# A hybrid decoder trunk on one core: constants first, x in pieces, merges in lockstep, and the second recurrence carried into the output projection

## The chip, the cores and the metric

The kernel runs on one core of one Trainium2 chip. The metric is the time of one execution in microseconds (us). TensorE (PE) multiplies matrices, PEld is its weight load, VectorE (DVE), ScalarE (ACT) and GpSimd (POOL) are the vector engines, and SyncE (SP) issues every DMA of this kernel. Each engine works off its own list of instructions in order.

## What is computed

Two layers over x of 1024 tokens by 1024 features, all float32, and a final RMSNorm. Cut to what matters:

```python
def hybrid_layer(x, ...):
    h = rms_norm(x, norm1_g)
    proj = h @ w_in              # q, k, v, z (4 heads of 128), b, a (4 + 4), short conv (3 x 512)
    qkv = silu(causal_depthwise_conv(qkv, dn_conv_w))
    q, k = l2_normalize(q), l2_normalize(k)
    beta, g = sigmoid(b_in), -exp(dn_a_log) * softplus(a_in + dn_dt_bias)
    o_dn = chunk_gated_delta_rule(q, k, v, g, beta)
    o_dn = o_dn * rsqrt(mean(o_dn * o_dn) + EPS) * dn_norm_g * silu(z)
    y = gate_b * causal_depthwise_conv(gate_c * hv, sc_conv_w)
    o_sc = y * rsqrt(mean(y * y, per group) + EPS) * sc_norm_g
    x = x + concatenate([o_dn, o_sc]) @ w_out
    h2 = rms_norm(x, norm2_g)
    return x + (silu(h2 @ w_gate) * (h2 @ w_up)) @ w_down      # 2816 wide
```

The gated delta rule runs over chunks of tokens one after the other: each step needs the state S that the step before it left.

## The kernel before

Activations lie transposed, features on partitions, tokens in two halves of 512. Every large product is made of three matmuls of 512 columns (`mm3`, L186): each operand is split into a rounded part hi (a cast, mostly on ACT) and the rest lo (a subtraction on DVE or POOL), and hi by hi, lo by hi and hi by lo are summed. So each weight block and each activation tile has to pass two engines before PE may use it.

A layer goes through these stages. The input projection takes head 0's k, q and v of half 0, then the decay inputs `ba` (tile ba_ps), then half 1, then heads 1, z of heads 0 and 1, the short convolution (`sconv`, products csc, hsc and bsc), heads 2 and 3, more `sconv`, z of heads 2 and 3. In layer 0 the second half of x is transposed (`x_half1`, tile xtp) and normed before `ba`, in one piece. Per head and half `gram` makes two products (gk, gq) and the tiles U and A; `value_tok` turns v round (vtok). A group of two heads is then a job: `invert` inverts small triangular blocks on DVE, DMAs carry them through DRAM, `merge` (rp, yp) puts the blocks together, `chain` runs four recurrence steps per half for its two heads (kS, TR, SU, op), `finish` norms and `gate` multiplies with z and stores the result to `od`.

Jobs run beside the projections: a job is a generator, `spawn` starts it with a lag, and `tick`, called at each matmul of a projection, moves it on when its lag is over. Then comes `drain()`, which runs all jobs to their end, and the output projection `po`: its operands are read back from DRAM (`ot`, and `rb`, the short convolution's norm factors, from `rd`), multiplied (L999) and split into `hhi_o` (ACT, L1000) and `hlo_o` (DVE, L1001), 8 tiles for each half of the tokens. After half 0's eight output blocks the second norm (sp_n, rr_n, bc) scales eight tiles xh (DVE, L1043) and splits them into hi_hP (ACT) and lo_hP (POOL) for the first two of the seven products P1 to P7 by which gate, up and down projections are made. Then half 1.

What stands on an engine in which order is decided by a list scheduler from the program's order, the pools' buffers (the `ot` tiles have 4) and dependencies.

Of the kernel before, what the change touches and what calls it, by code (L numbers as in the profile page):

```python
# [17 lines left out]
P = 128  # L18
# [10 lines left out]
LAG, TOK_LAG, SC_LAG, INV_LAG, GATE_LAG = 6, 36, 30, 110, 10  # L29
# [22 lines left out]
def tile_hybrid(ctx, tc, x, norm1_g, w_in, dn_conv_w, dn_a_log, dn_dt_bias, dn_norm_g,  # L52
# [18 lines left out]
          "Y": 4, "ub": 1, "yb": 1, "tb": 1, "X": 1, "R": 2, "rr0": 1, "rr1": 1, "vn0": 1, "vn1": 1, "St": 6}  # L71
# [159 lines left out]
    def w_in_early(l):  # L231
# [21 lines left out]
    xts = []  # L253
    for c in range(4):
        xt = sb(("ub", "yb")[c], f"xt_{c}", (P, D)) if c < 2 else \
            ring.tile([P, D], F32, tag=("whi", "wlo")[c - 2], bufs=3, name=f"xt_{c}")
        dma(xt, x[0, c * P:(c + 1) * P, :])
        xts.append(xt)
    split_early = w_in_early(0)
# [9 lines left out]
    xp = [[None, None] for _ in range(4)]
    for c in range(4):  # L270
        for kk in range(2):
            xp[c][kk] = sb(("k", "q")[kk], f"xp_{c}_{kk}")
            dma(xp[c][kk], x[0, HALF + c * P:HALF + (c + 1) * P, kk * HALF:(kk + 1) * HALF])
# [17 lines left out]
    for st, cst, n in ((st1, cst1, n_st1), (st2, cst2, n_st2)):  # L291
        ps = ps_("aux", "cps")
        PE.transpose(ps[:, :n], st, ident[:n, :n])
        V.tensor_copy(cst, ps[:, :n])
# [5 lines left out]
    def x_half1():  # L300

        s2x = sm.tile([P, 4, 2], F32, tag="ss1", bufs=1, name="ss1_1")
        for c in range(4):
            for kk in range(2):
# [24 lines left out]
    for l in range(DEPTH):  # L329

        if True:
# [21 lines left out]
            def ba():  # L353
# [3 lines left out]
                tp2 = fx(f"ba_tp{nm}", (P, NC, 16))  # L357
                for half in range(2):
# [5 lines left out]
                    S.copy(rows, ps)  # L364
                    for c in range(4):
                        PE.transpose(tp2[:, half * 4 + c, :], rows[:, c * P:(c + 1) * P], ident[:16, :16])
# [42 lines left out]
                V.tensor_scalar(neta, neta, -1.0, None, ALU.mult)  # L409

# [68 lines left out]
            def sumsq(ps, dst, nm):  # L479

                sq = sb("sqp", f"sq{nm}", sh4)
# [124 lines left out]
            def merge(hd, half, slot):  # L606

                nm = f"{l}_{hd}_{half}"
                U = units[hd, half]["U"]
# [4 lines left out]
                dma(Y, full_ap(yd[slot]))  # L614

                rp = aux(f"rp32_{nm}", (P, 4, 32))
# [8 lines left out]
                yp = aux(f"yp32_{nm}", (P, 2, 4, 32))  # L625
# [10 lines left out]
                rp = aux(f"rp64_{nm}", (P, 4, 64))  # L636
# [5 lines left out]
                yp = aux(f"yp64_{nm}", (P, 4, 64))  # L642
# [7 lines left out]
            def chain(g, half):  # L650
# [60 lines left out]
                yield GATE_LAG  # L711
                for hd in hds:
                    gate(hd, half)
# [51 lines left out]
            def sc_norm():  # L765
# [4 lines left out]
                r = rsqrt(m, [P, 32], f"r_{nm}", "s")  # L770
# [494 lines left out]
```

## Time and profile before

| what | value |
|---|---|
| median of 3 runs | 2458.01 us (2455.85 to 2458.72) |
| profiled execution: its time, its span | 2455.2 us, 2453.5 us |
| PE busy, share of the span | 2351.7 us, 96% |
| DVE, ACT, POOL busy | 1650.9, 915.9, 747.2 us |
| mean granted clock of TensorE | 0.985 |

The span is the time from the first to the last instruction. A granted clock of 1.00 is 2.4 GHz, 0.50 is 1.2 GHz. Matmuls are pipelined, so a busy PE is not a PE at its peak.

### The profile page before, as it was taken

Reading aid. Unit: us, or ns where it says so; the run is one execution under the profiler, and the core shown is the slowest. Engines: PE = TensorE matmul, PEld = TensorE weight load, DVE = VectorE, ACT = ScalarE, POOL = GpSimd, SP = SyncE. Lnnn points to the kernel's source line nnn. Section 1 sums busy time; section 2 is a strip of 40 time slices with the busy share of each in tenths; the row PEclk is TensorE's granted clock in tenths of the full one; section 3 lists DMA queues with packets and bytes.
Section 4 is the critical chain, followed back from the end, with each engine's and each line's share of the span. In section 5 each row is a group of like instructions: output and inputs, shape, how many; then the busy total and the mean of one; then the engine's idle time right before and its main releaser. Section 6 shows DMA issues by size and latency. Waiting matters only on the chain.

```text
span 2453.5 us, 31881 instructions
## 1 busy us (share of the span) xinstructions
PE 2351.7 (96%) x11522; PEld 1908.7 (78%) x11522; DVE 1650.9 (67%) x2786; ACT 915.9 (37%) x1933; POOL 747.2 (30%) x556
## 2 busy tenths in 40 slices
PE   6999999998999999899999999999999999999998
PEld 4787787786888888677867778888778888877777
DVE  7775763668566566797767666646776666568974
ACT  6524523434323223333344244244432232333334
POOL 3000000034454453456321001000445455434470
PEclk8999999999999999999999999999999999999999
DMA  7222222752342333644322312337324233255431
GB/s 225 72 62 75 64 68 82 224 155 64 100 129 91 111 110 96 205 142 140 116 69 72 73 48 69 75 105 243 104 86 129 90 104 111 92 179 167 134 120 69
DMA packets 360086, 274.16 MB, mean 112 GB/s; under 512 B 47310, under 2 KB 293368, under 8 KB 359928
## 3 DMA queue, kind: packets, MB, share of 16 engines
q1 hardware_dynamic: 359928, 272.13, 36.5%
q8 instruction: 90, 1.47, 0.3%
q14 instruction: 68, 0.56, 0.1%
HBM read 197.03 MB, written 75.04 MB: 111 GB/s over the span
## 4 chain that ended last, share of the span: by engine, by line
PE 77%; DVE 8%; issue 6%; DMA 3%; ACT 3%; POOL 2%; SPq 1%; POOLq 0%; DVEq 0%; ACTq 0%
PE P_g L186 16%; PE P_u L186 15%; PE P_d L186 10%; PE po L186 6%; PE ps_csc L186 4%; PE ps_bsc L186 4%; PE ps_hsc L186 4%; PE pd L186 3%; PE ps_q L186 2%; PE ps_v L186 2%; PE ps_z L186 2%; PE ps_k L186 2%; DMA stP<-hs_P 1%; POOL lo_dP L874 1%; DVE lo_hP L874 1%
## 5 line engine op out<-in xcount | busy, mean ns | idle before, releaser
L186 PE MATMUL P_g<-lo_hP,hiP_g 128*128 128x512 f32 x616 | 241.7, 393 | 8.5 <-DVE lo_hP L874 6.5
L186 PE MATMUL P_u<-hi_hP,hiP_u 128*128 128x512 f32 x616 | 241.8, 393 | 6.9 <-ACT hiP_u L898 6.9
L186 PE MATMUL P_g<-hi_hP,hiP_g 128*128 128x512 f32 x616 | 240.6, 391 | 1.3 <-ACT hiP_g L898 1.3
L186 PE MATMUL P_u<-lo_hP,hiP_u 128*128 128x512 f32 x616 | 241.2, 391 | 0.0
L186 PE MATMUL P_u<-hi_hP,loP_u 128*128 128x512 f32 x616 | 241.1, 391 | 0.0
L186 PE MATMUL P_g<-hi_hP,loP_g 128*128 128x512 f32 x616 | 240.1, 390 | 0.0
L186 PE MATMUL P_d<-lo_dP,hiP_d 128*128 128x512 f32 x504 | 202.5, 403 | 17.5 <-POOL lo_dP L874 14.6
L186 PE MATMUL P_d<-hi_dP,hiP_d 128*128 128x512 f32 x504 | 202.4, 403 | 9.5 <-ACT hi_dP L873 6.9
L186 PE MATMUL P_d<-hi_dP,loP_d 128*128 128x512 f32 x504 | 199.0, 396 | 1.6 <-DVE loP_d L899 1.6
L1173 DVE TENSOR_TENSOR xT<-P_d,xT 128x512 f32<-128x512 f32 x192 | 127.0, 682 | 50.7 <-PE P_d L186 48.5
L874 POOL TENSOR_TENSOR lo_hP<-xh,hi_hP 128x512 fp32r<-128x512 f32 x24 | 37.2, 1576 | 383.8 <-ACT hi_hP L873 383.8
L186 PEld LDWEIGHTS P_g<-lo_hP,hiP_g 128*128 128x128 f32 x616 | 115.9, 188 | 38.2 <-DVE lo_hP L874 11.0
L186 PEld LDWEIGHTS P_u<-hi_hP,hiP_u 128*128 128x128 f32 x616 | 116.7, 189 | 32.3 <-ACT hiP_u L898 7.8
L186 PEld LDWEIGHTS P_g<-hi_hP,hiP_g 128*128 128x128 f32 x616 | 115.9, 188 | 27.1 <-ACT hiP_g L898 2.2
L186 PEld LDWEIGHTS P_u<-lo_hP,hiP_u 128*128 128x128 f32 x616 | 116.8, 190 | 24.4
L186 PEld LDWEIGHTS P_u<-hi_hP,loP_u 128*128 128x128 f32 x616 | 116.5, 189 | 24.2
L186 PEld LDWEIGHTS P_g<-hi_hP,loP_g 128*128 128x128 f32 x616 | 115.9, 188 | 23.3
L186 PEld LDWEIGHTS P_d<-lo_dP,hiP_d 128*128 128x128 f32 x504 | 97.6, 194 | 46.0 <-POOL lo_dP L874 19.9
L186 PEld LDWEIGHTS P_d<-hi_dP,hiP_d 128*128 128x128 f32 x504 | 97.6, 194 | 36.2 <-ACT hi_dP L873 10.7
L898 ACT CAST hiP_g<-m_g 128x1024 fp32r<-128x1024 f32 (+1 forms) x66 | 60.1, 910 | 175.2 <-PE P_g L186 100.7
L898 ACT CAST hiP_u<-m_u 128x1024 fp32r<-128x1024 f32 (+1 forms) x66 | 60.1, 911 | 170.7 <-PE P_u L186 87.8
L186 PEld LDWEIGHTS P_d<-hi_dP,loP_d 128*128 128x128 f32 x504 | 96.5, 191 | 22.2 <-DVE loP_d L899 2.8
(393 smaller groups left out, 6069.1 us busy)
## 6 DMA issues: line engine op xcount, KB each, us to landing
stP<-hs_P SPq DMA_DIRECT2D x126, 256.0 KB, 3.8
m_g<-in_ffn_w_gate_dram SPq DMA_DIRECT2D x44, 512.0 KB, 3.9
m_u<-in_ffn_w_up_dram SPq DMA_DIRECT2D x44, 512.0 KB, 3.9
hs_P<-t SPq DMA_DIRECT2D x72, 256.0 KB, 2.2
m_d<-in_ffn_w_down_dram SPq DMA_DIRECT2D x48, 384.0 KB, 3.7
hs_P<-c_u SPq DMA_DIRECT2D x70, 256.0 KB, 2.4
raw_o<-in_w_out_dram SPq DMA_DIRECT2D x32, 512.0 KB, 4.8
xd<-xT SPq DMA_DIRECT2D x32, 256.0 KB, 2.4
```

Of the source, the lines that this page charges most:

```text
L186: last_mm[0] = PE.matmul(ps, lhsT=w(k)[i], rhs=m(k)[j], start=k + i + j == 0, stop=k + i == n).ins
L874: eng.tensor_tensor(res[1], src, res[0].bitcast(F32), ALU.subtract)
L898: S.copy(hi, src)
L1173: V.tensor_tensor(t, ps, t, ALU.add)
```

## The change

The constants' seven DMAs are issued ahead of x and their two transposes (cps) stand first on PE. The second half of x is loaded ahead of the first v weight, and `x_half1` is a job that moves on between projection matmuls. The first k weight's lo part is made on DVE in place of POOL. `ba` becomes a job behind half 0 of head 0. Both halves' `gram` come before `value_tok`. `merge` of the two heads of a group runs in lockstep, each with its own bank. `gate` is spawned with a lag of 40. `sconv(1)` moves ahead of head 2, `sconv(2)` and `sconv(3)` behind head 3. `drain()` moves from the end of the input projection to a place between the halves of the output projection, whose matmuls now tick the jobs, and the operands of half 1 (`load_os(1)`) are made behind it. In the first step of gate and up the products' order changes.

```diff
-LAG, TOK_LAG, SC_LAG, INV_LAG, GATE_LAG = 6, 36, 30, 110, 10
+LAG, TOK_LAG, SC_LAG, INV_LAG, GATE_LAG = 6, 36, 30, 114, 40
...
-          "Y": 4, "ub": 1, "yb": 1, "tb": 1, "X": 1, "R": 2, "rr0": 1, "rr1": 1, "vn0": 1, "vn1": 1, "St": 6}
+          "Y": 4, "ub": 1, "yb": 1, "tb": 1, "X": 2, "R": 2, "rr0": 1, "rr1": 1, "vn0": 1, "vn1": 1, "St": 6}
...
-        for c0, name, eng in ((512, f"k{l}_0", G), (0, f"q{l}_0", G), (1024, f"v{l}_0", G)):
+        for c0, name, eng in ((512, f"k{l}_0", V), (0, f"q{l}_0", G), (1024, f"v{l}_0", G)):
+            if between and len(raws) == 2:
+                between()
             t = ring.tile([P, KD, P], F32, tag="raw", bufs=3, name=f"raw_{name}")
...
-    xts = []
-    for c in range(4):
-        xt = sb(("ub", "yb")[c], f"xt_{c}", (P, D)) if c < 2 else \
...
-    split_early = w_in_early(0)
     dma(st1[0:DEPTH * 8, :], norm1_g.rearrange("l (k p) -> (l k) p", p=P))
...
+    xts = []
+    for c in range(4):
...
+    def load_half1():
+        for c in range(4):
+            for kk in range(2):
+                xp[c][kk] = sb(("k", "q")[kk], f"xp_{c}_{kk}")
+                dma(xp[c][kk], x[0, HALF + c * P:HALF + (c + 1) * P, kk * HALF:(kk + 1) * HALF])
+
+    split_early = w_in_early(0, load_half1)
...
+    for st, cst, n in ((st1, cst1, n_st1), (st2, cst2, n_st2)):
+        ps = ps_("aux", "cps")
+        PE.transpose(ps[:, :n], st, ident[:n, :n])
...
-    def x_half1():
+    def x_half1(hs):
...
+                yield 5
...
+        yield 10
+        hs[1] = make_h(lambda k: xT[1][k], r, lambda k: c_norm1(0, k), ps_("fx", "bc_n1_0_1"), "n1_0_1")
...
+                    rows2.append(rows)
+                return ba_rest(nm, rows2)
+
+            def ba_rest(nm, rows2):
+
...
+                for half in range(2):
+                    decay(0, half)
...
+                mb = (aux, fx)[hd % 2]
...
+                yield 14
+
+                rp = mb(f"rp32_{nm}", (P, 4, 32))
                 for c in range(4):
...
-                yield GATE_LAG
                 for hd in hds:
-                    gate(hd, half)
+                    spawn(call(gate, hd, half), GATE_LAG)
...
+                yield 16
...
+                if l + hd == 0:
+                    x_job = spawn(x_half1(hs), 8)
...
-                            hs[1] = x_half1()
-                        ba()
-                        decay(0, 0)
-                    if ty == "v" and hd + half > 0:
+                            while x_job in jobs:
+                                move(x_job)
...
-                        value_tok(hd, half)
-                        yield 24
+                        yield 8
                     if group is not None:
                         spawn(group, 0)
+                    for half in range(2):
+                        value_tok(hd, half)
+                        yield 12
...
-                    for hd in (2 * g, 2 * g + 1):
-                        yield from merge(hd, half, (hd % 2) * 2 + half)
+                    for lag in zip(*[merge(hd, half, (hd % 2) * 2 + half) for hd in (2 * g, 2 * g + 1)], strict=True):
+                        yield lag[0]
...
+            sconv(1)
             head(2, None)
             head(3, group(1))
-            for g in range(1, 4):
-                sconv(g)
-            spawn(call(sc_norm), SC_LAG + 12)
+            sconv(2)
+            sconv(3)
+            spawn(sc_norm(), SC_LAG + 12)
             w = [split_w(wcols(1536 + hd * P), f"z{l}_{hd}") for hd in (2, 3)]
...
-            drain()
...
-            for half in range(2):
+
+            def load_os(half):
...
+            load_os(0)
...
+                if half == 1:
+                    drain()
+                    load_os(1)
...
-                    mm3(ps, lambda k: (wo[0][:, korder[k], :], wo[1][:, korder[k], :]), lambda k: os_[half][k], KD)
+                    mm3(ps, lambda k: (wo[0][:, korder[k], :], wo[1][:, korder[k], :]), lambda k: os_[half][k], KD, tick)
...
-                        for it in (p0, p0, p1, p0, p1, p1):
+                        for it in (p0, p0, p0, p1, p1, p1):
...
-                    for qs in (("P1", "P2"), ("P5",), ("P6",), ("P7",), ("P3",), ("P4",)):
-                        if qs[0] in ("P4",):
-                            last_opnds(qs[0])
+                    for qs in (("P1", "P2"), ("P5", "P6"), ("P7", "P3", "P4")):
                         for m in mats[:2]:
                             for q in qs:
+                                if q == "P4" and m is mats[0]:
+                                    last_opnds(q)
                                 m.step(q)
                 elif i > 1:
...
```

**What the order of instructions shows.** Three places.

On PE, layer 0, where half 0 of the output projection ends (po_0_7 is its last block, po_1_0 the first of half 1; sp_n is the second norm's sum), the order of before goes on like this:

```order
L186 MATMUL po_0_7_4961<-hhi_o_0_7_4604,lo_o_7_4882 128x512
L864 MATMUL sp_n_0_0_4992<-ones_83,acc_0_0_4690 128x1
L186 MATMUL po_1_0_5078<-hhi_o_1_0_4610,hi_o_8_4919 128x512
L186 MATMUL po_1_0_5078<-hlo_o_1_0_4611,hi_o_8_4919 128x512
L186 MATMUL po_1_0_5078<-hhi_o_1_0_4610,lo_o_8_4920 128x512
L186 MATMUL po_1_0_5078<-hhi_o_1_1_4616,hi_o_8_4919 128x512
```

There po_1_0 needs hhi_o_1 and hlo_o_1, which DVE made while half 0's first four blocks ran. In this piece one sp_n is followed by half 1 at once. After the change eight sp_n and four bc stand between po_0_7 and po_1_0 on PE, and on DVE at the same place the operands of half 1 come behind the norm of half 0 (rsqrt, then eight scalings xh, of which the last five stand here):

```order
L1072 SCALAR_TENSOR_TENSOR xh_0_6_4555<-xh_0_6_4555,cst_88,bc_0_4958 128x512
L1072 SCALAR_TENSOR_TENSOR xh_0_1_4550<-xh_0_1_4550,cst_88,bc_0_4958 128x512
L1072 SCALAR_TENSOR_TENSOR xh_0_3_4552<-xh_0_3_4552,cst_88,bc_0_4958 128x512
L1072 SCALAR_TENSOR_TENSOR xh_0_5_4554<-xh_0_5_4554,cst_88,bc_0_4958 128x512
L1072 SCALAR_TENSOR_TENSOR xh_0_7_4556<-xh_0_7_4556,cst_88,bc_0_4958 128x512
L1026 SCALAR_TENSOR_TENSOR hlo_o_1_0_5004<-ot_1_0_5005,cst_89,hhi_o_1_0_5003 128x512
L1026 SCALAR_TENSOR_TENSOR hlo_o_1_1_5010<-ot_1_1_5011,cst_89,hhi_o_1_1_5009 128x512
L1026 SCALAR_TENSOR_TENSOR hlo_o_1_2_5016<-ot_1_4_5017,cst_89,hhi_o_1_2_5015 128x512
L1026 SCALAR_TENSOR_TENSOR hlo_o_1_3_5025<-ot_1_5_5026,cst_89,hhi_o_1_3_5024 128x512
L1024 TENSOR_TENSOR ot_1_6_5035<-ot_1_6_5035,rb_1_6_5037 128x512
```

All of half 1's operands have moved from the middle of half 0 to behind its scaling; on ACT the eight casts hi_hP stand ahead of the first hhi_o_1 likewise. The last four `ot` of half 1 are loaded into the buffers of the first four, and layer 1 has the same order.

On DVE, layer 0, before the change, the second half's normed tiles (ht_n_0_1) come behind the convolution of v (y_v, vT_v):

```order
L461 SCALAR_TENSOR_TENSOR y_v_0_0_579<-pre_v_0_0_576,cst_88,y_v_0_0_579 128x512 x3
L464 SCALAR_TENSOR_TENSOR vT_v_0_0_574<-pre_v_0_0_576,y_v_0_0_579 128x512
L211 SCALAR_TENSOR_TENSOR ht_n_0_1_0_702<-xT_0_245,cst_88,bc_n_0_1_695 128x512
L211 SCALAR_TENSOR_TENSOR ht_n_0_1_1_708<-xT_1_246,cst_88,bc_n_0_1_695 128x512
L211 SCALAR_TENSOR_TENSOR ht_n_0_1_2_714<-xT_2_247,cst_88,bc_n_0_1_695 128x512
L213 TENSOR_TENSOR hlo_n_0_1_0_701<-ht_n_0_1_0_702,hhi_n_0_1_0_700 128x512
```

After the change the ht_n_0_1 have moved ahead of it, to behind q's; the last of them and what follows:

```order
L211 SCALAR_TENSOR_TENSOR ht_n_0_1_5_691<-xT_5_256,cst_88,bc_n_0_1_654 128x512
L211 SCALAR_TENSOR_TENSOR ht_n_0_1_6_697<-xT_6_257,cst_88,bc_n_0_1_654 128x512
L213 TENSOR_TENSOR hlo_n_0_1_4_684<-ht_n_0_1_4_685,hhi_n_0_1_4_683 128x512
L211 SCALAR_TENSOR_TENSOR ht_n_0_1_7_703<-xT_7_258,cst_88,bc_n_0_1_654 128x512
L213 TENSOR_TENSOR hlo_n_0_1_6_696<-ht_n_0_1_6_697,hhi_n_0_1_6_695 128x512
L477 COPY halocv_0_744<-pre_v_0_0_745 128x3
L479 SCALAR_TENSOR_TENSOR y_v_0_0_748<-pre_v_0_0_745,cst_88,y_v_0_0_748 128x512
L472 COPY pre_q_0_1_914<-halocq_0_631 128x3
L479 SCALAR_TENSOR_TENSOR y_v_0_0_748<-pre_v_0_0_745,cst_88,y_v_0_0_748 128x512 x2
```

On PE, layer 0, in the output projection's second block (po_0_1), the change puts the second group's recurrence of half 1 (TR, SU, op, kS of heads 2 and 3) and the short convolution's transposed norm (rt_sc):

```order
L697 MATMUL TR_2_1_0_4344<-rr_2_1_0_4318,Y_2_1_4148 128x128
L697 MATMUL TR_3_1_0_4348<-rr_3_1_0_4323,Y_3_1_4153 128x128
L792 MATMUL rt_sc_4369<-ident,y_r_sc_4298 32x128
L186 MATMUL po_0_1_4659<-hhi_o_0_0_4477,lo_o_1_4546 128x512
L705 MATMUL SU_2_1_0_4358<-vn_2_1_0_4346,kdec_2_1_2775 128x128
```

So one matmul of po_0_1 stands between pieces of the recurrence here. Before, all four heads' recurrence and rt_sc stood ahead of the first po matmul.

## Rows read from the trace of the kernel before

**Rows 1.** Windows (us): busy time and instructions of each engine, granted clock, DMA.

```profile
core 0: us, PE busy (x) PEld busy (x) DVE busy (x) ACT busy (x) POOL busy (x), PEclk, DMA share, GB/s
0.00:26.00 26.00, 10.31 (x55) 9.77 (x55) 17.88 (x50) 12.52 (x31) 11.06 (x19) 0.80 0.86 259
...
47.00:64.00 17.00, 12.29 (x43) 4.68 (x43) 12.28 (x17) 7.52 (x19) 5.48 (x4) 0.80 0.33 123
...
200.00:300.00 100.00, 95.50 (x691) 76.00 (x690) 65.32 (x174) 52.90 (x192) 4.80 (x9) 0.98 0.21 57
...
375.00:450.00 75.00, 74.44 (x575) 59.53 (x575) 33.42 (x105) 28.29 (x111) 0.00 (x0) 1.00 0.31 90
...
504.60:518.90 14.30, 14.30 (x76) 12.04 (x75) 11.14 (x24) 7.95 (x13) 5.61 (x5) 1.00 0.32 101
```

**Rows 2.** Waits of PE, 0 to 65 us: us in total, times, longest.

```profile
PE cps L293 <- DMA xp<-in_x_dram: 5.7, 1, 5.7
PE cps L293 <- DMA st<-in_dn_conv_w_dram: 5.0, 1, 5.0
```

**Rows 3.** Timeline of the start: start us, us, engine, line, operation, xcount [idle before].

```profile
10.95 0.42 SPq L262 DMA_DIRECT2D st<-in_dn_conv_w_dram  x1
11.98 2.35 POOL L177 TENSOR_TENSOR lo_k<-raw_k,hi_k 128x1024 fp32r<-128x1024 f32 x1 [0.63 <-ACT hi_k L176]
12.03 2.32 DVE L155 TENSOR_TENSOR t_n<-y_n 128x4 f32<-128x4 f32 x1
14.47 5.69 DVE L156 TENSOR_TENSOR t_n<-t_n,rr_n 128x4 f32<-128x4 f32 x1
25.89 0.49 PE L186 MATMUL ps_k<-hhi_n,hi_k 128*128 128x512 f32 x1
```

**Rows 4.** Timeline of PE, 94 to 99 us.

```profile
98.15 0.66 PE L488 MATMUL vtok<-ident,vT_v 128*128 128x128 f32 x4 [2.77 <-DVE U L565]
```

**Rows 5.** Waits of PE, 1225 to 1330 us (layer 1).

```profile
PE vtok L488 <- DVE U L565: 4.5, 1, 4.5
PE ps_k L186 <- POOL lo_k L177: 2.4, 1, 2.4
```

**Rows 6.** Timeline of DVE, ACT, POOL and PE around 504 to 530 us.

```profile
505.68 1.23 DVE L177 TENSOR_TENSOR lo_o<-raw_o,hi_o 128x1024 fp32r<-128x1024 f32 x1 [0.20 <-ACT hi_o L176]
...
511.53 5.36 DVE L1043 SCALAR_TENSOR_TENSOR xh<-xh,cst,bc 128x512 f32<-128x512 f32 x8 [1.31 <-PE bc L1039]
...
517.40 2.09 DVE L177 TENSOR_TENSOR lo_o<-raw_o,hi_o 128x1024 fp32r<-128x1024 f32 x1
...
513.90 3.74 ACT L873 CAST hi_hP<-xh 128x512 fp32r<-128x512 f32 x7
...
514.60 11.24 POOL L874 TENSOR_TENSOR lo_hP<-xh,hi_hP 128x512 fp32r<-128x512 f32 x7 [0.28 <-ACT hi_hP L873]
...
511.25 0.48 PE L186 MATMUL po<-hhi_o,lo_o 128*128 128x512 f32 x1
```

**Rows 7.** Groups of PE instructions, 504.6 to 518.9 us: xcount, busy us, mean ns, idle.

```profile
L186 PE MATMUL po<-hhi_o,lo_o 128*128 128x512 f32 x18 | 7.1, 395 | 0.0
...
L864 PE MATMUL sp_n<-ones,acc 128*128 128x1 f32 x8 | 1.4, 240 | 0.0
```

**Rows 8.** Tile ot, 440 to 525 us: duration ns min/median/max, and its DMAs' landing.

```profile
L1000 ACT ACTIVATE hhi_o<-ot,cst x16: 707/723/727, 440.9 to 479.5; 128x512 fp32r<-128x512 f32 x16
L1001 DVE SCALAR_TENSOR_TENSOR hlo_o<-ot,cst,hhi_o x16: 737/746/755, 442.4 to 480.2; 128x512 fp32r<-128x512 f32 x16
...
DMA to landing us min/median/max: 3.9/5.2/6.3
```

**Rows 9.** Tile rb, 440 to 525 us: its DMAs' landing.

```profile
DMA to landing us min/median/max: 4.2/4.2/4.2
```

**Rows 10.** Waits of PE, 551 to 610 us.

```profile
PE P_u L186 <- ACT hiP_u L898: 3.5, 1, 3.5
```

**Rows 11.** Window of 571.7 to 578.5 us, columns as in the first group.

```profile
571.70:578.50 6.80, 5.54 (x13) 4.39 (x14) 5.56 (x5) 2.71 (x4) 6.80 (x5) 0.50 0.00 0
```

More of the change, by code (lines that the diff above doesn't have):

```diff
@@ L229, in w_in_tile, with w_in_early @@
         return pre_w.pop(key)
-    def w_in_early(l):
+    def w_in_early(l, between=None):
         raw = sm.tile([P, KD, 8], F32, tag="ba_raw", bufs=1, name=f"raw_ba{l}")
@@ L266, in tile_hybrid @@
     dma(st2[DEPTH * 17:, :], final_norm_g.rearrange("(k p) -> k p", p=P))
+    xts = []
+    for c in range(4):
+        xt = sb(("ub", "yb")[c], f"xt_{c}", (P, D)) if c < 2 else \
+            ring.tile([P, D], F32, tag=("whi", "wlo")[c - 2], bufs=3, name=f"xt_{c}")
+        dma(xt, x[0, c * P:(c + 1) * P, :])
+        xts.append(xt)
+    xp = [[None, None] for _ in range(4)]
+    def load_half1():
[4 more added lines that the diff above has]
+    split_early = w_in_early(0, load_half1)
     dma(alog, bass.AP(dn_a_log.tensor, dn_a_log.offset, [[0, P], [NH, DEPTH], [1, NH]]))
     dma(dtb, bass.AP(dn_dt_bias.tensor, dn_dt_bias.offset, [[0, P], [NH, DEPTH], [1, NH]]))
[L269 to L273, printed above, removed]
+    for st, cst, n in ((st1, cst1, n_st1), (st2, cst2, n_st2)):
+        ps = ps_("aux", "cps")
+        PE.transpose(ps[:, :n], st, ident[:n, :n])
+        V.tensor_copy(cst, ps[:, :n])
     XTB = ("ch0", "ch1", "o0", "o1")
@@ L290, in tile_hybrid @@
                 V.tensor_copy(xT[0][kk * 4 + k][:, c * P:(c + 1) * P], ps[:, k, :])
[L291 to L294, printed above, removed]
     split_early()
@@ L356, in ba @@
                 wba = pre_w.pop((l, "ba"))
-                tp2 = fx(f"ba_tp{nm}", (P, NC, 16))
+                rows2 = []
                 for half in range(2):
@@ L364, in ba @@
                     S.copy(rows, ps)
+                    rows2.append(rows)
+                return ba_rest(nm, rows2)
+            def ba_rest(nm, rows2):
+                tp2 = fx(f"ba_tp{nm}", (P, NC, 16))
+                for half in range(2):
                     for c in range(4):
-                        PE.transpose(tp2[:, half * 4 + c, :], rows[:, c * P:(c + 1) * P], ident[:16, :16])
+                        PE.transpose(tp2[:, half * 4 + c, :], rows2[half][:, c * P:(c + 1) * P], ident[:16, :16])
                 tph = sm.tile([P, NC, 8], F32, tag="ba_tph", bufs=1, name=f"ba_tph{nm}")
@@ L396, in ba @@
                 V.scalar_tensor_tensor(y, y, -1.0, alog[:, l:l + 1, :].broadcast_to(sh), ALU.mult, ALU.mult)
+                yield 44
                 gps = fx(f"gps{nm}")
@@ L399, in ba @@
                 V.tensor_copy(gcum, gps[:, :32].rearrange("p (c h) -> p c h", h=NH))
+                yield LAG
                 gtp = fx(f"gtp{nm}", (32, HALF))
@@ L415, in spawn @@
                 jobs.append([lag, gen])
+                return jobs[-1]
             def move(job):
@@ L479, in sumsq @@
             def sumsq(ps, dst, nm):
-                sq = sb("sqp", f"sq{nm}", sh4)
+                sq = sb("y", f"sq{nm}", sh4)
                 for c in range(4):
@@ L614, in merge @@
                 dma(Y, full_ap(yd[slot]))
-                rp = aux(f"rp32_{nm}", (P, 4, 32))
+                yield 14
+                rp = mb(f"rp32_{nm}", (P, 4, 32))
                 for c in range(4):
@@ L624, in merge @@
                 yield LAG
-                yp = aux(f"yp32_{nm}", (P, 2, 4, 32))
+                yp = mb(f"yp32_{nm}", (P, 2, 4, 32))
                 for c in range(4):
@@ L635, in merge @@
                 yield LAG
-                rp = aux(f"rp64_{nm}", (P, 4, 64))
+                rp = mb(f"rp64_{nm}", (P, 4, 64))
                 for c in range(4):
@@ L641, in merge @@
                 yield LAG
-                yp = aux(f"yp64_{nm}", (P, 4, 64))
+                yp = mb(f"yp64_{nm}", (P, 4, 64))
                 for c in range(4):
@@ L789, in head @@
                         if l == 0:
-                            hs[1] = x_half1()
-                        ba()
-                        decay(0, 0)
-                    if ty == "v" and hd + half > 0:
+                            while x_job in jobs:
+                                move(x_job)
+                        spawn(ba(), 8)
+                    if ty == "v" and hd > 0:
                         decay(hd, half)
@@ L805, in finish @@
                         gram(hd, half, (hd % 2) * 2 + half)
-                        value_tok(hd, half)
-                        yield 24
+                        yield 8
                     if group is not None:
                         spawn(group, 0)
+                    for half in range(2):
+                        value_tok(hd, half)
+                        yield 12
                 spawn(finish(), TOK_LAG)
```

5 lines of the change are left out of this document (removed).

## The prediction

> **What bounds the kernel now.** I read the page first, then windows by stage, then PE's waits in each stage, then the timeline of the places that the order changes. PE is busy for 2351.7 of 2453.5 us, so only what PE waits for, runs through at the low clock, or loses by mixing small matmuls into large ones can be won or lost; every matmul of 512 columns of before is still there after. The windows [rows 1] show where that is. From 0 to 26 us PE is busy for 10.3, from 47 to 64 for 12.3 at a mean granted clock of 0.80, from 200 to 300 (the first group's merges and recurrence) for 95.5 at 0.98, and from 375 to 450 (second group) for 74.4 of 75. From 504.6 to 518.9 us, where the output projection passes from half 0 to half 1, PE is busy for all of 14.3 us. That last row is the one to keep in mind: there nothing was left to win.
>
> **The loss: half 1 of the output projection.** The order shows that half 1's operands hhi_o and hlo_o, made in the middle of half 0 before, now stand behind half 0's scaling on DVE and behind its casts on ACT. What these took is in the trace [rows 6]: the eight scalings end at 511.53 + 5.36 = 516.9 us, and the casts at 513.90 + 3.74 = 517.6, with a weight cast between them that now comes earlier, so some 517.5. Then the first hhi_o takes 0.72 and the first hlo_o 0.75 us [rows 8]: half 1 starts at 518.2 with its first matmul and goes on at 519.0. What PE did meanwhile in before is the 14.3 us of [rows 1]; of that only the norm remains as work for the gap, two groups like sp_n at 1.4 us and the four transposes bc, at most another 1.4 at the same rate [rows 7], and less by their starts, since the ends overlap. I take 2.8 for all three. So 14.3 - 2.8 = 11.5 us of matmuls are pushed back. DVE and ACT work before that point is not less than before, so nothing shortens the chain.
>
> A second wait follows. The `ot` tiles have four buffers, so the last four of half 1 are issued only when the first four are split, the first at 519.0. Landing took 3.9 us at least and 5.2 in the median [rows 8], then come the product with rb (as long as a scaling, 5.36 / 8 = 0.67), 0.72 and 0.75: 525.0. PE has four tiles' matmuls until about 522, paced by hlo_o at 0.75 each. That is a wait of 3 us; if the landings contain time spent behind the stores of od, it could be near nothing, and by the median it is 4.4. I take 2.
>
> The clock is third. In the first gate and up block PE waited 3.5 us at once [rows 10] and then stood at 0.50, 1.2 GHz, for 6.8 us [rows 11], which costs half of the work done in it, 2 to 3.4 us. A gap of 11 us will do no less; I take 2. Together 15.5 us in each layer, 31 in all; bounds 11.5 and 20 per layer.
>
> **The gains.** *Start.* The first projection matmul comes at 25.89 us [rows 3], behind two waits of PE for 5.7 and 5.0 us [rows 2], which are the transposes of constants that were queued behind x and the first weights. The same stretch has two DVE operations on 128x4 tiles that took 2.32 and 5.69 us [rows 3] where the tiles hold four elements per partition, while POOL made lo_k and then lo_q. With the constants first, x starts later by seven issues of about 0.42 us [rows 3], 2.9. The rsqrt is free of lo_k, and neither cps wait remains. If the two held operations become short (together 0.3 instead of 8.0), the first matmul comes at 25.89 - 7.7 + 2.9 = 21.1. What can hold it beyond that: lo_q and lo_v still run on POOL, and ACT now does the eight squares of x's second half ahead of the first cast, which need that half landed. If these cost all that was won, it stays at 25.9. I take 22.7, nearer to the lower end, since one of three lo's is gone and no PE wait is left: a gain of 3.2. Next, `ba` of half 1 waited for ht_n, made behind v's convolution: 17 - 12.3 = 4.7 us idle between 47 and 64, and about 2.6 us through the low clock (5.2 us of busy PE at 0.5) [rows 1]. The order moves these ht_n ahead of the convolution, so most goes: I take 5.8 of 7.3. Start: 9 (3 to 12).
>
> *Gram.* PE waited 2.77 us for U before vtok in layer 0 [rows 4] and 4.5 in layer 1 [rows 5]. With both grams first, eight matmuls between and vtok last, about half to two thirds goes: 1.3 and 3. Layer 1's wait of 2.4 for lo_k shrinks when DVE makes it in 1.23 instead of POOL in 2.35 [rows 3, 5, 6]: 1. Together 5.3 (0 to 8).
>
> *First group.* Idle 4.5 us and 2% of the clock in 100 us [rows 1], some 6.5 us per layer that could go. In lockstep each head's small merge matmuls cover the other's copies, but the steps still wait for DVE and ACT, which now also carry `sconv`. I take 4 per layer (0 to 8), 8 in all, layer 1 like layer 0.
>
> *Second group.* PE idles 0.56 us only [rows 1]. Fewer changes between small and large matmuls can be won: the first large one behind a small one took 0.48 us instead of 0.395 [rows 6, 7], so 0.09 each, and some 3 us per layer with the steps' own waits. Against it: rt_sc now stands beside the recurrence's half 1, and three recurrence steps later po needs the factors that go from rt_sc through rd to rb. A landing of rb took 4.2 us [rows 9], the store ahead of it at least half as much, then 0.67 + 0.72 + 0.75: about 9 us. The three steps are 30 small products of heads 2 and 3; at one or two passes of 1.4 / 8 = 0.18 [rows 7] that is 5 to 10 us. A new wait of 0 to 4, I take 2. Net 1 per layer, 2 in all (-3 to 5 per layer).
>
> *Gate and up.* The wait of 3.5 [rows 10] is for a weight cast that the new order needs later, but P6 needs scaled tiles of both halves that DVE makes one after the other anyway. 1 per layer, 2 in all (-2 to 4). The lags, the second X buffer, `sc_norm` in two steps and the sumsq tiles only shift jobs that PE's projections cover: nothing.
>
> **Sum.** Gains 9 + 5.3 + 8 + 2 + 2 = 26.3, loss 31: 4.7 us slower. On the profiled execution, 2455.2 us, that is 2459.9; it lies 2.8 below the median 2458.0, against which the change is timed: 2462.7, say 2463.
>
> **The rivals.** *Faster: the lockstep runs at PE's pace.* If two interleaved heads leave PE no wait, both groups give back idle time, clock and most changes: 6.5 + 0.56 + 4 = 11 per layer instead of 5. That is 12 us better, 2451. It decides from about 10 us per layer. For it: per step the two heads have work for PE almost all the time, and the second group already idles next to nothing. Against: `sconv` shares DVE and ACT.
>
> *Slower: the recurrence queues behind sconv.* The four steps of the first half have no projection matmul among them after the change. Each step needs three small DVE or ACT operations in turn; if one in each step stands behind a 128x1024 operation of 1.2 us [rows 6], eight steps lose up to 10 us per layer, and a typical loss of 5 in place of a gain of 4 gives 2463 + 2 x 9 = 2481.
>
> *Slower: hlo_o held by POOL.* In before lo_o took 1.23 us alone and 2.09 while POOL ran lo_hP, from 514.6 to 525.8 [rows 6]. The ten DVE operations of half 1's operands now fall in just that stretch. At 0.86 more each for five to eight of them half 1's start is paced by DVE: 4 to 6 us per layer, 2473. The Trainium skill, SBUF — State Buffer, section "SBUF: two separate sides", says that VectorE and GpSimd hold a shared port pair as an exclusive lock, the loser blocked for the whole instruction. By that rule each of the ten could wait out a lo_hP of 1.6 us [rows 6], 16 us per layer and 2490; the row shows 0.86 over an operation twice as long, so the trace agrees that it happens, and only in part.
>
> *The loss doesn't come* is a rival only if half 1's operands could overtake the scaling; the trace's rows of DVE follow its order, so I give it no share of its own.
>
> **How the numbers follow.** Forecast 0.40 (2455 to 2471), faster rival 0.30 (2441 to 2453), sconv 0.10 (2474 to 2486), POOL 0.17 (2468 to 2480), others 0.03, two thirds of it faster by a better start. A change of 0.2%, 4.9 us, is about what a measurement tells here from none, so the bounds are 2453.1 and 2462.9. Of the forecast 0.18 lies within them and 0.22 above; the other cases lie on one side. So faster 0.30 + 0.02 = 0.32, same 0.18, slower 0.22 + 0.10 + 0.17 + 0.01 = 0.50. The range goes from 2442, near the lower end of the faster rival, to 2482, into sconv's, and leaves out about a tenth on each side.
>
> **What would show it.** After po_0_7 of half 0 PE should stand idle for about 12 us in both layers, released by hlo_o, with the clock at 0.50 behind it, and a shorter wait for ot follows. The first ps_k should come near 22.7 us, `ba` be done near 53. The rb wait should show in po's first block, the first group's stretch have less idle. Wrong I would be if PE has other work in that gap, or if the groups take much less time than taken here.

## The result and the profile after

The changed kernel took 2517.53 us (median of 4 runs, 2510.48 to 2524.08) against 2458.1 of before on the same chip: ratio 1.0243, 95% interval 1.0215 to 1.0271. It is slower by 59 us where 5 were forecast, and lies outside the range. The profiled execution took 2517.63 us, 62.4 more than the one of before.

The page after, its span and the engines' busy time:

```profile
span 2515.9 us, 31886 instructions
## 1 busy us (share of the span) xinstructions
PE 2377.5 (94%) x11522; PEld 1930.6 (77%) x11522; DVE 1663.8 (66%) x2788; ACT 914.7 (36%) x1933; POOL 748.5 (30%) x554
```

The work is the same, 11522 PE instructions, so the 62 us are waits and low clock. Where they come from is read by counting: both kernels have 9112 matmuls of 512 columns, and the start of the one behind the first n in one timeline less that in the other says how far the changed kernel is behind at that point. It is a running difference, so a step between two rows is the cost of what lies between; inside a stretch where small matmuls stand in another place it jumps to and fro, so only marks outside are given.

| n-th matmul, what ends there | before | after | behind | step |
|---|---|---|---|---|
| 192, head 0 | 85.9 | 83.3 | -2.6 | -2.6 |
| 576, z of heads 0 and 1, sconv(0) | 188.1 | 189.2 | 1.1 | 3.7 |
| 1152, first group | 373.5 | 372.1 | -1.4 | -2.5 |
| 1536, second group, most of po half 0 | 497.3 | 504.9 | 7.6 | 9.0 |
| 1600, gap between the halves | 514.7 | 539.2 | 24.4 | 16.8 |
| 1920, first gate and up block | 604.1 | 634.7 | 30.6 | 6.2 |
| 5120, rest of layer 0, start of layer 1 | 1390.9 | 1419.3 | 28.4 | -2.2 |
| 5696, first group of layer 1 | 1576.3 | 1602.2 | 25.9 | -2.5 |
| 6080, second group | 1699.3 | 1737.5 | 38.2 | 12.3 |
| 6144, gap | 1716.7 | 1771.7 | 55.0 | 16.8 |
| 6528, first gate and up block | 1820.6 | 1882.0 | 61.4 | 6.4 |
| 9088, end | 2433.3 | 2495.8 | 62.5 | 1.1 |

Three places cost, each in both layers: the gap (33.6 together), the second group (21.3), the first gate and up block (12.6). The start and the first groups gave little. The windows of after (columns as in [rows 1]) show the state of PE in them:

```profile
0.00:26.00 26.00, 10.67 (x47) 8.55 (x48) 15.43 (x54) 17.07 (x42) 8.34 (x18) 0.85 0.91 293
...
400.00:475.00 75.00, 70.60 (x528) 55.91 (x527) 35.01 (x96) 26.82 (x97) 0.00 (x0) 0.91 0.37 115
...
512.30:526.60 14.30, 3.91 (x25) 3.47 (x23) 9.10 (x22) 7.05 (x12) 5.18 (x5) 0.64 0.26 80
526.60:538.00 11.40, 10.11 (x27) 5.95 (x28) 10.55 (x10) 4.49 (x7) 6.06 (x4) 0.70 0.33 92
...
575.00:640.00 65.00, 52.43 (x211) 40.03 (x210) 57.94 (x75) 25.84 (x38) 28.19 (x18) 0.87 0.16 49
```

In the second group's stretch PE is busy for 70.6 of 75 us at a clock of 0.91; in the like stretch of before it was busy for 74.4 at 1.00 [rows 1]. In the gap PE is busy for 3.9 of 14.3 us. PE's waits over the whole span, the ones that are new or have grown:

```profile
PE po L186 <- ACT hhi_o L1025: 17.1, 6, 6.7
PE P_g L186 <- DVE lo_hP L898: 14.2, 6, 2.9
...
PE P_g L186 <- ACT hi_hP L897: 8.2, 6, 3.3
PE bc_n L205 <- DVE rowr_n L199: 7.0, 1, 7.0
PE ktok L506 <- DVE U L583: 6.1, 3, 2.1
...
PE ps_z L186 <- DVE z_z L740: 4.6, 4, 1.4
PE gk L582 <- DVE U L583: 4.5, 2, 2.9
PE vtok L506 <- DVE U L583: 3.8, 4, 1.0
...
PE ps_k L186 <- ACT ba_rows L370: 3.0, 1, 3.0
```

The wait for rowr_n stands ahead of the first projection matmul, and those for U are 14.4 us together where before had 7.8. The timeline around the gap in layer 0 (columns as in [rows 3]) answers to [rows 6]:

```profile
512.36 0.69 DVE L1056 TENSOR_TENSOR xh<-po,xo 128x512 f32<-128x512 f32 x1 [2.71 <-PE po L186]
...
519.94 5.36 DVE L1072 SCALAR_TENSOR_TENSOR xh<-xh,cst,bc 128x512 f32<-128x512 f32 x8 [2.23 <-PE bc L1068]
...
525.86 2.56 ACT L1025 ACTIVATE hhi_o<-ot,cst 128x512 fp32r<-128x512 f32 x4
...
526.61 6.61 DVE L1026 SCALAR_TENSOR_TENSOR hlo_o<-ot,cst,hhi_o 128x512 fp32r<-128x512 f32 x4 [1.31 <-ACT hhi_o L1025]
...
534.61 2.74 DVE L1026 SCALAR_TENSOR_TENSOR hlo_o<-ot,cst,hhi_o 128x512 fp32r<-128x512 f32 x4 [0.19 <-ACT hhi_o L1025]
...
521.42 11.24 POOL L898 TENSOR_TENSOR lo_hP<-xh,hi_hP 128x512 fp32r<-128x512 f32 x8 [173.96 <-ACT hi_hP L897]
...
526.63 0.79 PE L186 MATMUL po<-hhi_o,hi_o 128*128 128x512 f32 x1 [6.72 <-ACT hhi_o L1025]
...
534.63 0.49 PE L186 MATMUL po<-hhi_o,hi_o 128*128 128x512 f32 x1 [0.36 <-ACT hhi_o L1025]
```

Half 1 starts at 526.6, 14.3 us after DVE took up the last block of half 0 at 512.4. Then four hlo_o take 6.61 us, 1.65 each instead of 0.746 [rows 8]: POOL runs lo_hP until 532.7, and behind that the last four take 2.74, 0.69 each. The wait for ot that follows is 0.36 us.

And the start (columns the same):

```profile
16.84 2.75 POOL L177 TENSOR_TENSOR lo_q<-raw_q,hi_q 128x1024 fp32r<-128x1024 f32 x1 [2.86 <-ACT hi_q L176]
...
17.29 2.32 DVE L160 TENSOR_TENSOR t_n<-t_n,h_n 128x4 f32<-128x4 f32 x1
...
23.63 0.80 PE L186 MATMUL ps_k<-hhi_n,hi_k 128*128 128x512 f32 x1 [1.49 <-ACT hhi_n L212]
...
59.13 0.80 PE L186 MATMUL ps_k<-hhi_n,hi_k 128*128 128x512 f32 x1 [3.04 <-ACT ba_rows L370]
...
97.21 2.07 PE L582 MATMUL gk<-kT_k 128*128 128x128 f32 x8 [2.88 <-DVE U L583]
```

An operation of the rsqrt still takes 2.32 us, beside lo_q now; `ba` is through without a stall, but the next projection waits 3.0 us until ACT, which is at v's silu, has copied ba_rows out of PSUM; and the second half's gk waits for the first half's U.

Where the second group's merges stand now, in z, the timeline of ACT and DVE reads:

```profile
407.25 0.60 ACT L738 ACTIVATE th_z<-ps_z 128x512 f32<-128x512 f32 x1 [4.57 <-PE ps_z L186]
414.93 0.55 ACT L643 ACTIVATE R<-rp 32x128 f32<-32x128 f32 x2 [7.09 <-PE rp L640]
415.50 0.60 ACT L738 ACTIVATE th_z<-ps_z 128x512 f32<-128x512 f32 x1
...
416.13 0.69 DVE L740 SCALAR_TENSOR_TENSOR z_z<-th_z,ps_z 128x512 f32<-128x512 f32 x1 [7.57 <-ACT th_z L738]
```

ACT is idle for 7 us, then does the merge's R, which needs PE's rp, and only then z's th_z, which frees the bank that PE's next z needs. (Matmuls write to PSUM; a bank is here one of the two PSUM tiles that the projections take in turn.)

### The profile page after: what moved, and what is told of

It is laid out like the page before. It is cut to its first block, busy times and chain, and to the rows that moved or that the text cites. A ratio compares the mean times of both kernels' runs of the same rounds, so it can differ in the third digit from the quotient of the medians.

```text
span 2515.9 us, 31886 instructions
## 1 busy us (share of the span) xinstructions
PE 2377.5 (94%) x11522; PEld 1930.6 (77%) x11522; DVE 1663.8 (66%) x2788; ACT 914.7 (36%) x1933; POOL 748.5 (30%) x554
## 4 chain that ended last, share of the span: by engine, by line
PE 73%; DVE 12%; issue 8%; ACT 3%; DMA 2%; POOL 2%; SPq 0%; DVEq 0%; POOLq 0%; ACTq 0%
PE P_g L186 16%; PE P_u L186 16%; PE P_d L186 10%; PE po L186 6%; PE ps_hsc L186 3%; PE ps_bsc L186 3%; PE ps_csc L186 3%; PE ps_z L186 3%; PE pd L186 3%; PE ps_q L186 2%; DVE lo_dP L898 1%; PE ps_k L186 1%; DVE y_k L479 1%; DVE xh L1072 1%; POOL lo_dP L898 1%
## 5 line engine op out<-in xcount | busy, mean ns | idle before, releaser
L186 PE MATMUL P_g<-lo_hP,hiP_g 128*128 128x512 f32 x616 | 245.6, 399 | 16.3 <-DVE lo_hP L898 14.2
L186 PE MATMUL P_d<-lo_dP,hiP_d 128*128 128x512 f32 x504 | 202.5, 403 | 16.3 <-POOL lo_dP L898 13.3
L186 PEld LDWEIGHTS P_g<-hi_hP,hiP_g 128*128 128x128 f32 x616 | 117.3, 190 | 35.7 <-ACT hi_hP L897 11.5
L186 PEld LDWEIGHTS P_u<-hi_hP,loP_u 128*128 128x128 f32 x616 | 115.6, 188 | 24.1
L186 PEld LDWEIGHTS P_d<-hi_dP,hiP_d 128*128 128x128 f32 x504 | 97.4, 193 | 38.4 <-ACT hi_dP L897 12.6
L186 PE MATMUL po<-hhi_o,hi_o 128*128 128x512 f32 x256 | 102.8, 405 | 17.1 <-ACT hhi_o L1025 17.1
```

Source lines behind the costliest of these rows:

```text
L186: last_mm[0] = PE.matmul(ps, lhsT=w(k)[i], rhs=m(k)[j], start=k + i + j == 0, stop=k + i == n).ins
```

## The experiments

How far each run's trace is behind the kernel before at the marks, in us:

| run | 192 | 576 | 1152 | 1536 | 1600 | 1920 | 5120 | 5696 | 6080 | 6144 | 6528 | 9088 |
|---|---|---|---|---|---|---|---|---|---|---|---|---|
| changed kernel | -2.6 | 1.1 | -1.4 | 7.6 | 24.4 | 30.6 | 28.4 | 25.9 | 38.2 | 55.0 | 61.4 | 62.5 |
| operands early | 1.7 | 5.3 | 2.9 | 13.0 | 13.0 | 17.0 | 12.1 | 9.7 | 20.0 | 20.0 | 24.1 | 22.8 |
| drain before po | 2.2 | 5.2 | 1.2 | 10.3 | 10.3 | 14.3 | 9.9 | 7.5 | 16.1 | 16.1 | 20.6 | 17.5 |
| old product order | 0.1 | 3.1 | -0.8 | 7.3 | 24.2 | 24.2 | 20.7 | 18.3 | 30.1 | 47.0 | 48.0 | 46.1 |
| sconv(1) back | -2.5 | 1.2 | 0.5 | -0.1 | 16.8 | 23.5 | 20.9 | 20.4 | 20.6 | 37.4 | 44.2 | 42.2 |
| start alone | -2.7 | -0.2 | -0.2 | -0.5 | -0.5 | -0.5 | -3.9 | -3.8 | -3.8 | -3.8 | -3.8 | -4.2 |
| sconv(1) alone | 2.0 | 3.5 | -0.5 | 15.3 | 15.3 | 16.3 | 17.1 | 13.2 | 21.2 | 21.2 | 21.5 | 22.8 |
| three repairs | -2.7 | -0.4 | -2.2 | -2.7 | -2.7 | -2.7 | -6.5 | -7.2 | -7.3 | -7.3 | -6.4 | -6.7 |
| and old gram | -0.5 | 3.5 | 0.0 | 0.6 | 0.6 | 0.6 | -2.7 | -6.1 | -5.1 | -5.1 | -5.1 | -6.6 |
| product order alone | 0.6 | 0.9 | 0.9 | 0.8 | 0.8 | 7.6 | 7.2 | 7.2 | 7.0 | 7.0 | 11.0 | 9.7 |
| start, lo_q on DVE | -1.1 | 1.5 | 2.9 | 2.5 | 2.5 | 3.4 | -2.2 | -2.3 | -2.1 | -2.1 | -2.2 | -2.6 |
| start and lockstep | -2.8 | -0.3 | -0.8 | -2.2 | -2.2 | -2.2 | -7.5 | -8.1 | -7.2 | -7.2 | -6.2 | -5.8 |
| repairs, old drain | -0.6 | 1.9 | -2.4 | -2.2 | -2.1 | -2.1 | -5.4 | -8.1 | -7.1 | -7.1 | -6.3 | -6.9 |

The first column shows how far one execution is from another: the ten kernels with the changed kernel's start stand between -2.8 and 2.2 there, on the mean at -1.0. Steps further on repeat within about 2 us: the changed kernel and the first three experiments, whose input projections are the same, have 9.0, 10.1, 9.1 and 8.1 at the second group of layer 0.

**Half 1's operands early** (on the changed kernel):

```diff
                 for d in range(KD):
+                    if half == 0 and d == 4:
+                        drain()
+                        load_os(1)
...
-                if half == 1:
-                    drain()
-                    load_os(1)
```

> The changed kernel with one edit: all jobs are run to their end and half 1's operands are made ahead of the fifth output block of half 0, not behind half 0's scaling. Theory (the gap between the halves costs 17 us per layer by the order of DVE and ACT): the gap closes, 2517.5 - 2 x 17 = 2484 us, with half 1's first matmul within 1 us of half 0's last. If the later wait in the first gate and up block (6 us per layer) is a consequence of the gap, it goes as well: 2472. Rival (the gap was short of DVE and POOL time, not of order: the shared port): part of the 17 us stays and 2495 or more results.

Measured: 2473.3 us, ratio to before 1.0064 (1.0045 to 1.0084). The step from 1536 to 1600 is 0.0 instead of 16.8, in both layers. The window from the end of half 0 on:

```profile
517.50:532.00 14.50, 14.50 (x76) 12.18 (x75) 11.28 (x24) 8.08 (x13) 5.74 (x5) 1.00 0.31 99
```

76 instructions fill it, just as in before [rows 1]. So the gap is shown to be a matter of the order on DVE and ACT. The step in gate and up falls from 6.2 and 6.4 to 4.0 and 4.1. That a third of it followed from the gap isn't shown: the order of products alone, with no gap, costs 6.8 and 4.0 further down.

**Drain before the output projection:**

```diff
                 for i in range(2):
                     zproj(2 + i, half, w[i])
+            drain()
...
             load_os(0)
+            load_os(1)
...
-                if half == 1:
-                    drain()
-                    load_os(1)
```

and the output projection's `mm3` without `tick`.

> The changed kernel with the recurrence run to its end ahead of the output projection, both halves' operands made there and no jobs moved by its matmuls, as in the kernel before. If the second group's 9 to 12 us per layer come from running on into the output projection, they go with the gap: 2517.5 - 2 x (17 + 10) = 2463. If they come from where its merges now stand (in z), only the gap goes, 2484, and the tail of the recurrence without any projection beside it may add to it.

Measured: 2484.76 us, 1.0115 (1.0076 to 1.0154); its four runs spread from 2471.76 to 2495.3, the profiled one is the fastest. The gap goes; the second group's step stays at 9.1 and 8.6 us. So the run into the output projection is not the main cost there.

**Old product order:**

```diff
-                        for it in (p0, p0, p0, p1, p1, p1):
+                        for it in (p0, p0, p1, p0, p1, p1):
...
-                    for qs in (("P1", "P2"), ("P5", "P6"), ("P7", "P3", "P4")):
+                    for qs in (("P1", "P2"), ("P5",), ("P6",), ("P7",), ("P3",), ("P4",)):
+                        if qs[0] in ("P4",):
+                            last_opnds(qs[0])
```

> The changed kernel with the order of the products in the first gate and up step, and of the parts that are fetched ahead, as before. Theory (the new order asks for P6 right behind P5, before DVE has scaled and split both halves): the 6 us per layer in the first gate and up block go, 2505. Rival (they follow from the gap ahead of half 1): unchanged, 2517.

Measured: 2502.07 us, 1.0185 (1.0166 to 1.0204). The step in gate and up falls from 6.2 and 6.4 to 0.0 and 1.0. The order of the products and that in which their weight parts are fetched changed together, here and in every other run, so which of the two costs stays open.

**sconv(1) back behind head 3:**

```diff
-            sconv(1)
             head(2, None)
             head(3, group(1))
+            sconv(1)
             sconv(2)
```

> The changed kernel with the short convolution's group 1 back behind head 3. Theory (with sconv(1) ahead of head 2 the second group of the recurrence starts 133 projection matmuls later, in z, where few matmuls and two PSUM banks stand between its steps and the end): its 9 to 12 us per layer go, 2517.5 - 2 x 10 = 2497, and its merges stand in the short convolution again. Rival (the lockstep or the later gates cost it): unchanged within 4 us, 2517.

Measured: 2496.51 us, 1.0164 (1.014 to 1.0187). The second group's step is -0.6 and 0.2 instead of 9.0 and 12.3. Its stretch, again in the short convolution, runs at full clock:

```profile
375.00:420.00 45.00, 43.77 (x424) 34.67 (x423) 19.80 (x64) 14.91 (x67) 0.00 (x0) 1.00 0.28 81
```

**The start alone** (on the kernel before; constants first, x in pieces, lo_k on DVE, `ba` as a job, as in the diff of the change).

> The kernel before with the start of the change alone: constants first, second half of x in pieces, first k weight's lo on DVE, the decay inputs as a job. In the changed kernel the start is 1.5 to 2.6 us ahead in layer 0 and nothing in layer 1, with a wait of 3 us of PE for ba_rows and a norm operation held for 2.3 us on DVE. If that is the start's own doing it shows here as well: 2 to 3 us faster, 2454. If the start lost through the other parts, the forecast's 9 us come: 2447.

Measured: 2452.44 us, 0.998 (0.9967 to 0.9993), of which -2.7 stand at the end of head 0. They are gone at 576, where this kernel waits 4.1 us for U before vtok, more than the 2.77 of [rows 4]; what it gains comes in layer 1. The 9 us do not come even with nothing else changed.

**sconv(1) alone** (on the kernel before):

```diff
+            sconv(1)
             head(2, None)
             head(3, group(1))
-            for g in range(1, 4):
+            for g in range(2, 4):
                 sconv(g)
```

> The kernel before with sconv(1) moved ahead of head 2 and nothing else. Theory (this move pushes the second recurrence into z and behind, and that is what cost): 10 to 20 us slower, 2466 to 2476, the more since here all jobs must end ahead of the output projection. Rival (it takes the lockstep or the later drain as well): within 4 us of before.

Measured: 2472.34 us, 1.0063 (1.0043 to 1.0083), with steps of 15.8 and 8.0 us at the second group. Its window where the step of layer 0 arises:

```profile
450.00:475.00 25.00, 22.70 (x164) 16.51 (x163) 8.69 (x18) 6.25 (x17) 0.00 (x0) 0.61 0.37 122
```

The clock was 0.61 of full speed. The move costs by itself, without lockstep, later gates or a later drain. At the first group it gains 4.0 and 3.9 us.

**Three repairs**, the edits of the first, third and fourth experiment together on the changed kernel.

> The changed kernel with three repairs at once: half 1's operands early, the old product order, sconv(1) behind head 3. If the three causes add up: 2517.5 - 44 - 21 - 8 (what is left of the product order when the gap is gone) = 2444 to 2451, faster than before by 0.2 to 0.5%. If they overlap (the second group's chain, earlier again, or the gap's repair having taken part of it): 2455 to 2465.

Measured: 2452.35 us, 0.9978 (0.9967 to 0.9989). The 59 us of loss are gone and 5 more. The median lies 1 us above the range that was expected if the three causes add up, and below that for an overlap; nothing else of size is left. It is also where the start alone stands, so the rest of the change adds nothing that shows beside it.

**And gram and value_tok in turn:**

```diff
-                        yield 8
+                        value_tok(hd, half)
+                        yield 24
                     if group is not None:
                         spawn(group, 0)
-                    for half in range(2):
-                        value_tok(hd, half)
-                        yield 12
```

> As the three repairs, and gram and value_tok of a half in turn again. Theory (both grams first make the second gk wait for the first U, because they share a bank, 3 us in layer 0 at the place where the trace shows it, and similar waits for heads 2 and 3): 3 to 8 us faster than the three repairs. Rival (the wait only moves from vtok to gk): within 3 us of them.

Measured: 2447.54 us, 0.9962 (0.9949 to 0.9976). The medians differ by 4.8 us, but the intervals overlap and the traces end within 0.1 us of each other, since vtok waits 4.1 us where gk did 2.1. Not decided.

**Product order alone** (on the kernel before, the third experiment's edit the other way round).

> The kernel before with the new order of products in the first gate and up step and nothing else. The run with the gap closed still lost 4 us per layer there, the run with the old order gained 5.5 to 6. Theory (P6 and P7 are asked for before DVE can have them): 6 to 10 us slower, 2463 to 2467. Rival (only together with the gap): within 3 us of before.

Measured: 2468.76 us, 1.005 (1.0034 to 1.0065), with steps of 6.8 and 4.0 us. That is about 2 us above the expected range, and there is no gap here. Its waits of PE in that block, where before had 3.5 for hiP_u [rows 10] and 3.3 for lo_hP:

```profile
PE P_g L186 <- DVE lo_hP L874: 6.8, 3, 2.9
PE P_g L186 <- ACT hi_hP L873: 4.1, 3, 3.3
```

**The start with lo_q on DVE:**

```diff
-        for c0, name, eng in ((512, f"k{l}_0", V), (0, f"q{l}_0", G), (1024, f"v{l}_0", G)):
+        for c0, name, eng in ((512, f"k{l}_0", V), (0, f"q{l}_0", V), (1024, f"v{l}_0", G)):
```

> The start alone, with the first q weight's lo on DVE too instead of POOL. Theory (a DVE operation with two SBUF inputs waits while POOL's lo_q runs): the rsqrt step that took 2.32 us takes 0.15 to 0.2; DVE has 1.2 us more to do instead, so the first projection matmul comes 0 to 1 us earlier. Rival (it waited for something else, a DMA or ACT): the 2.32 us stay.

Measured: 2452.49 us, 0.9978 (0.9968 to 0.9987), the same as the start alone. The timeline:

```profile
17.36 0.16 DVE L160 TENSOR_TENSOR t_n<-t_n,h_n 128x4 f32<-128x4 f32 x1
17.44 1.22 DVE L177 TENSOR_TENSOR lo_q<-raw_q,hi_q 128x1024 fp32r<-128x1024 f32 x1
...
23.48 1.04 ACT L176 CAST hi_v<-raw_v 128x1024 fp32r<-128x1024 f32 x1 [1.18 <-DMA raw_v<-in_w_in_dram]
...
25.09 0.80 PE L186 MATMUL ps_k<-hhi_n,hi_k 128*128 128x512 f32 x1 [4.03 <-ACT hhi_n L212]
```

The held operation takes 0.16 us when POOL is free: that part holds. But the first matmul came 1.6 us later than in the start alone, not earlier: ACT's cast of v's weight (hi_v), which has to wait for its DMA, now stood ahead of the first hhi.

**Start and lockstep** (on the kernel before; `zip` over the two merges, a bank for each head, two X buffers).

> The kernel before with the start and with the merges in lockstep (own bank for each head, second X buffer), no other part. The forecast gave the lockstep 4 us per layer in the first group and 1 to 3 in the second: then 6 to 12 us faster than the start alone, 2441 to 2446. If lockstep only moves the waits: within 3 us of the start alone, 2451 to 2454.

Measured: 2450.33 us, 0.9966 (0.9955 to 0.9978), 2 us better than the start alone, with intervals that overlap. Over both groups the traces give -1.9 in layer 0 and 0.3 in layer 1, where the start alone gives -0.3 and 0.1. The lockstep is worth little.

**The repairs with the old drain:** the best kernel with the drain of the second experiment.

> The best repaired kernel (operands early, old product order, sconv(1) back, gram and value_tok in turn) with the jobs run to their end ahead of the output projection, as before. If running on into the output projection is worth something by itself, this is slower than 2447.5 by some us; if the second recurrence ends ahead of it anyway, it is the same within 3 us.

Measured: 2448.0 us, 0.9959 (0.9947 to 0.9972), the same as with the late drain. This doesn't settle what running on into the output projection is worth: with sconv(1) back the last TR of the recurrence stands about 100 projection matmuls ahead of it in both, so the late drain had no recurrence left to carry. Both best versions beat the kernel before by 0.4%.

## Why the prediction was wrong, step by step

*The gap was right.* 15.5 us per layer were forecast and 16.8 measured, and the matmuls start 14.3 us after the end of half 0 where 13.6 were worked out (504.6 to 518.2). Less the norm's 2.8 that is 11.5, as forecast, and 5.3 are left for what follows, where 2 for `ot` and 2 for the clock were taken. What followed the start was mis-told. The second wait, taken at 2 us for the last four ot, is 0.36; in its place the four hlo_o took 6.61 us, 3.6 more than at 0.746 each, while POOL ran lo_hP. This is the rival "hlo_o held by POOL", which came true inside the forecast's term and covered the wait for ot. The clock was low there too, 0.70 from 526.6 to 538.0, but hlo_o set the pace until 533.2, so how the 5.3 divide isn't shown; that the sum came near is in part luck. The Trainium skill, SBUF — State Buffer, "SBUF: two separate sides", has the port pair as an exclusive lock; 1.65 us for each hlo_o agrees with waiting out one lo_hP in turn, until POOL's eight are done. (The price by that rule was summed wrongly in the prediction: 16 us per layer on 2463 make 2495, not 2490. Four operations were held, not ten.) In the gap itself this was only read from the rows; at the start, the run with lo_q on DVE showed that such an operation, with two SBUF inputs, is held by POOL's lo and not by something else (2.32 to 0.16 us).

*The second group was the step that failed most.* The forecast was a net gain of 1 us per layer with -3 as its bound; measured were losses of 9.0 and 12.3. I read the order only for the wait that rb adds, and for the number of changes between small and large matmuls. What the same order also said, that the merges begin 133 projection matmuls later than before, in z, I gave no price. There is no sconv behind them there: the first steps of the merges stand with two or three matmuls of z between them, and in the stretch of 400 to 475 us PE idled 4.4 us and the clock was 0.91. Two experiments, from both sides, show that the place of sconv(1) is the cause; how its 9 to 12 us divide into waits and clock is read from these windows and not tried apart. Of the waits, 2.3 us per layer are z's, in two pieces. Before the second, of 0.9, ACT's small R copies stand ahead of z's own operation; the first, of 1.4 at 408.6, comes before any step of a merge. z had one bank there in place of two: the last product of sconv (bsc), done at 401.8, was read from its bank only at 437.5. sconv(1) alone loses 15.8 in layer 0 without any wait of z's, so these waits are the changed kernel's own and not what the move costs in general. The rb wait, for which I took 2 us, shows as 1.7 (layer 1: 1.4) and was about right.

*Gate and up failed by its sign.* I gave it a gain of 1 per layer (-2 to 4), because the wait for hiP_u would go. It went, and P_g waits for lo_hP and hi_hP, 14.2 and 8.2 us over both layers (6.5 and none before), with DVE busy for 58 of 65 us: P6 directly behind P5 asks for what DVE has not yet made, and the clock is 0.87 over the block. Before had this in layer 0:

```profile
PE P_g L186 <- DVE lo_hP L874: 3.3, 4, 1.1
...
551.00:615.00 64.00, 55.55 (x233) 42.68 (x232) 54.48 (x78) 26.30 (x39) 30.86 (x20) 0.95 0.22 70
```

I had written that argument down and still kept the gain. The order alone costs 6.8 and 4.0 us.

*The start* was given 9 us and has 2.6 in this trace, 1.0 on the mean of the ten. The first matmul at 23.6 (22.7 forecast) was near, though one wait for cps stayed (3.7 us in this trace) where none was to remain. `ba` lost its stall as forecast and ended at 56.1 (53 forecast), but a new wait of 3.0 for ba_rows took most of it, since ACT's copies stand behind v's silu. I named what is late next only for the first matmul, not for `ba`.

*Gram* was given 5.3 us in all; the step to 576 is 3.7 us of loss in layer 0. The wait moved from vtok to gk (2.88), and the clock fell behind it. But the start alone, with gram as it was, loses 2.5 at the same step, so at most a third is gram's own. Over the whole execution PE's waits for U rose: 14.4 us at gk, ktok and vtok, where before had them at vtok alone:

```profile
PE vtok L488 <- DVE U L565: 7.8, 4, 4.5
```

With vtok last, PE waits for U at what comes earlier, and no less.

*The first group* gained 2.5 per layer of 4, but the runs don't credit the lockstep, for which it was forecast: at the same step sconv(1) alone, without lockstep, gains 4.0 and 3.9, start and lockstep about 0.5 in each layer, and the changed kernel with sconv(1) back 0.7 and 0.5. With gram and value_tok in turn as well it is 3.5 and 3.4 again, so how the parts share it isn't settled; that the sign came right was luck. *The faster rival* fell: lockstep alone is worth 1 to 2 us in all, not 12, and that is not clear of the noise. *sconv's rival* fell too: the first half's four steps among sconv's operations lose nothing.

So the range was too narrow on one side: each term's loss bound was taken from rows of waits that were there before, and none from a stage that gets a new place.

## What to carry to other kernels

Where a job moves to another stage, price the stage it moves into: how many filler matmuls stand between its steps, and which operations of that stage queue behind the job's on each engine. Operands that a second loop needs should be asked for in the first loop's middle, not behind its closing norm: the engines work in order, and here it cost 17 us per layer. A new order of products helps only if the engine that makes their operands is ahead; with DVE nearly all busy it moves the wait and can lengthen it.

## What the runs showed of the hardware that was not expected

That POOL would hold the hlo_o was priced, at 0.86 us more each, and 0.90 was measured (1.65 instead of 0.746). Not expected was that the two take turns and that both pay. In the gap an hlo_o ends 0.55 us behind a lo_hP, the next lo_hP 1.13 behind the hlo_o, and so on; beside them a lo_hP takes 1.72 to 1.74 us instead of 1.28. The eight scalings xh, which read bc from PSUM and only xh as a full tile from SBUF, were not held beside the same lo_hP: 0.742 to 0.748 us each. And at the start an operation on 128x4 elements took 2.32 us instead of 0.16; it ended at 19.61, POOL's lo_q at 19.59.

In the window of sconv(1) alone the clock cost more than the waits: PE idled 2.3 of 25 us, and at 0.61 its 22.7 busy us are worth about 14 at full clock, an estimate from these two numbers.
